# Two-block transformer, one core: the order of the first block's mixers, its output gates and its merge

## The chip, the cores and the metric

The kernel runs on one core of a Trainium2 chip, as one launch. The metric is the device time in microseconds (us) from the first to the last instruction, with what lies around it, of one execution; before the change the median of three runs is 3106.4 us. Five engines work side by side, each through its own instruction list, strictly in the order in which the program wrote it: TensorE (PE; its weight loads are shown apart as PEld), VectorE (DVE), ScalarE (ACT), GpSimd (POOL) and SyncE (SP, which issues the transfers).

## The reference, cut to what matters

The program computes two blocks of two layers each on 256 latent tokens of width 1024; the first block carries 256 context tokens as well. The change touches the token mixers of the first block alone:

```python
def token_mixers(hx, hc, ...):
    cu, mqkv, mo, mg, aq, ak, av, bg = split(h @ w_in)       # for latent and context tokens
    conv  = conformer_conv(cu, ...)      # a * sigmoid(g), 31 taps along the tokens, layernorm over 512 channels, silu, @ w_o
    mlstm = mlstm_readout(mlstm_bidirectional(...), mo, ...) # 4 heads of 256; rmsnorm per head, * sigmoid(mo), @ w_o
    attn  = attend(q, [k_c, k_x], [v_c, v_x]) @ w_attn_out   # 8 heads, 2 key heads
    g_conv, g_mlstm, g_attn = split(sigmoid(bg))
    return (g_conv * conv + g_mlstm * mlstm + g_attn * attn) @ w_out
```

Layer 0 needs latent and context outputs (512 columns), layer 1 only the latent ones (256). All arithmetic is float32.

## The kernel before

**Products.** Every float32 operand of a product is split into a high and a low half (fp32r), and each product is three matmuls: high by high, low by high, high by low. `lin` (L409 to L420) does this for one output tile of 128 features: it takes the next 128x128 weight pair from a stream and issues the three matmuls L417, L418 and L419 for each of kt tiles of the inner dimension (eight for the width of 1024). Activations lie feature by feature: 128 features in the partitions, the tokens (512 or 256) in the columns. Weights come as 512 KB transfers (`raw`), ACT makes the high half (`wh`, L326) and DVE the low half (`wl`, L310), 128x1024 at a time. A stream's order in memory is the order in which `lin` takes it, so the host packs it by `ORDER`.

**One layer of mixers.** After the normalisation come the gate logits, attention's keys, values and queries; then the loop over `ORDER`, which alternates m and c: for m, one mLSTM head (`mlstm`), for c, one quarter of the convolution's 512 channels (`glu_conv`). Behind them come eight more `lin` calls for the output gates (`mlstm_gate`), and then the merges: for each branch, 16 `lin` calls in layer 0 (eight for the branch's output product, eight for its merge gate).

- *An mLSTM head.* Q and k by `lin`, the score products L458 to L460 (`aux<-mq,mk` and the like), v by `lin`; then the head's 512 or 256 columns go through two segments of 256 (one in layer 1). A segment takes its forward and backward direction through two value blocks (`pv<-mv,mEh`, L1379 to L1381: 21 or 30 matmuls each), which need the decayed scores: PE (row maxima, `aux<-msr,selr`, L1337), ACT (an exponential), DVE (`mE<-...` and the low half `mEl`). DVE or ACT then brings the block out of PSUM as `mh` with a reciprocal; ACT squares `mh`, POOL takes the power of the mean and scales `mh` (L1321), PE transposes it (`aux<-cst,mh`, L1327) and it is stored in `hs`. There is one PSUM buffer for `pv` and one of each of the score operands.
- *A convolution quarter.* Two `lin` calls, ACT's tanh, DVE's product `glu<-glu,mm`, and then 31 taps on DVE: one multiplication (L319) and 30 multiply-adds (`cv<-glu,p,cv`, L307), each on the sum that the one before left. `conv_norm` takes the mean and the variance over the four quarters: POOL sums, PE multiplies by a constant (`aux<-ss,cst`, L1184), DVE subtracts (`cv<-aux,cv`).
- *Attention.* Scores, a softmax (DVE maxima, ACT exponentials, POOL scaling) and the value products L1138 (`aux<-pT,va`), in `ao`.

**What sets the order.** The program is written out by Python generators. `self.queue(name, interval, depth, generator)` puts side work into a named queue; `tick(us)`, which `lin` calls with its own nominal time, gives every queue that credit, and each time it reaches the interval one step of the queue's generator is written. So the interval says how far apart the steps stand in the engines' lists. `flush(name)` writes what is left at once. `soon()` marks work that is to be written early. Before the change attention's queue has an interval of 15.9 in layer 0, the convolution's 6.4, and a queue `ogate` multiplies `hs` by the output gates. The merges come in the order attention, convolution (flushed first), mLSTM.

The lines of the profile that matter here: L417 to L419 `lin`; L307 multiply-adds on DVE; L310 two-tensor operations on DVE; L326 high halves and L304 other passes on ACT; L313 and L321 on POOL.

Of the kernel before, what the change touches and what calls it, by code (L numbers as in the profile page):

```python
# [24 lines left out]
AF = mybir.ActivationFunctionType  # L25
OP = mybir.AluOpType
# [5 lines left out]
KD = D // P  # L32
# [4 lines left out]
MH = 4  # L37
# [24 lines left out]
ORDER = [(kind, h) for h in range(MH) for kind in "mc"]  # L62
# [111 lines left out]
def _layout(inp):  # L174
# [12 lines left out]
    for l in range(DEPTH):  # L187
        w = a["w_in"][l]
# [7 lines left out]
        for kind, h in ORDER:  # L196
            if kind == "m":
                c = slice(h * 256, (h + 1) * 256)
                parts += [qkv[:, :1024][:, c], qkv[:, 1024:2048][:, c]]
            else:  # L200
                parts += [cu[:, h * P:(h + 1) * P], cu[:, 512 + h * P:512 + (h + 1) * P]]
        parts.append(mo)
# [15 lines left out]
        g = a["mlstm_gate_b"][l]  # L218
# [73 lines left out]
class _K:  # L292
# [561 lines left out]
    def mixers(self, l, st, xs, segs, nq, first):  # L854
# [5 lines left out]
        with ExitStack() as es:  # L860
# [4 lines left out]
            with tc.tile_pool(name=f"head{l}", bufs=1) as hp:  # L865
# [19 lines left out]
                for j in range(4):  # L885
                    for seg in segs:
                        self.queue("attn", (15.9 if l == 0 else 15) * slow, 2 if l == 0 else 1, self.attention(j, seg, seg * len(segs) // 2, kT, va, hp, ao))
                for kind, h in ORDER:
                    if kind == "m":
                        self.mlstm(l, h, st, xs, xq, segs, nq, rows, hp, hs)  # L890
                    else:
                        self.queue("conv", (6.4 if l == 0 else 8.7) * slow, 1,
                                   self.glu_conv(l, h, st, xq, segs, nq, mp, cv), early=False)
                self.queue("conv", (6.4 if l == 0 else 8.7) * slow, 1, self.conv_norm(l, nq, cv))
                for n in range(0, KD, G):
                    self.mlstm_gate(l, n, st, xq, nq, hs)
                for name in ("mlstm", "ogate", "attn"):
                    self.flush(name)
                if l == 0:
                    self.load_x()  # L900
            with tc.tile_pool(name=f"merge{l}", bufs=1) as gp:
                merged = gp.tile([P, KD, nq], F32, name="merged")
                for name, src, kt, b, first in (("wba", ao, 4, 2, True), ("wbc", cv, 4, 0, False),
                                                ("wbm", hs, 8, 1, False)):
# [301 lines left out]
    def mlstm(self, l, h, st, xs, xq, segs, nq, rows, hp, hs):  # L1206
# [26 lines left out]
        with self.soon():  # L1233
            S = [self.mlstm_scores(seg, i * 256, qT, kT, hp) for i, seg in enumerate(segs)]
        nc.gpsimd.tensor_copy(v[0][:, :, 256:258], self.onec[:, None, :].to_broadcast([P, 4, 2]))
# [13 lines left out]
        for i, seg in enumerate(segs):  # L1249
            self.queue("mlstm", (6.8 if l == 0 else 5.8), 2, self.mlstm_seg(h, seg, i * 256, nq, S[i], v, rows, hp, hs))  # L1250

# [13 lines left out]
    def mlstm_gate(self, l, n, st, xq, nq, hs):  # L1265

        G = 512 // nq
        bank = self.mmt()
        for i in range(G):
            self.lin(bank[:, i * nq:(i + 1) * nq], st["wi"], xq, KD)  # L1270
        t = self.tmp()
        with self.soon():
            self.act(t, bank, AF.Tanh, scale=0.5)
            for i in range(G):
                w = self.mnwh[l][:, n + i:n + i + 1]
                self.act(t[:, i * nq:(i + 1) * nq], t[:, i * nq:(i + 1) * nq], AF.Identity, scale=w, bias=w)

        def finish():
            if n // 2 == 3:
                self.flush("mlstm")  # L1280
            m = hs[:, n:n + G, :].rearrange("p g n -> p (g n)")
            self.tt(m, m, t, OP.mult)
            yield

        self.queue("ogate", (5.2 if l == 0 else 6.9), 1, finish())
# [15 lines left out]
    def mlstm_seg(self, h, seg, c0, nq, S, v, rows, hp, hs):  # L1301
# [27 lines left out]
        nc.scalar.copy(hs[:, 2 * h:2 * h + 2, c0:c0 + 256], pt.rearrange("p (e q) -> p e q", e=2))  # L1329
# [458 lines left out]
```

## Time and profile before

| | |
|---|---|
| median of 3 runs (lowest to highest) | 3106.4 us (3102.4 to 3106.88) |
| the profiled execution: time, span | 3104.9 us, 3103.1 us |
| PE busy | 3044.2 us, 98% of the span |
| DVE, ACT, POOL busy | 60%, 47%, 12% |
| PE's mean granted clock | 0.995 of full speed |
| layer 0's mixers, first block | about 110 to 467 us |
| layer 1's mixers, first block | about 1190 to 1460 us |

A row of a timeline gives the start, the duration, the engine, the line and the operation as out<-in; in brackets stand the engine's idle time before it and what released it. A row of the groups by line gives the count, the busy time, the mean duration of one, and the idle time before. PE's records are pipelined: one matmul starts before the record of the last has ended, so a pace is read from starts. Records of consecutive DVE instructions overlap a little as well. [...]

### The profile page before, as it was taken

How to read it: one execution, taken by the hardware profiler on the slowest of the kernel's cores; microseconds unless marked ns; L12 is line 12 of the kernel's file. 1: busy time of each engine (PE TensorE's matmuls, PEld its weight loads, DVE VectorE, ACT ScalarE, POOL GpSimd, SP SyncE). 2: the span in 40 equal slices, each digit the busy share in tenths (PEclk: the TensorE clock that was granted, in tenths of full speed). 3: DMA queues.
4: the chain of work that ended last, by engine and by line, in shares of the span. 5: the costliest groups of instructions: out<-in, count | busy, mean ns of one | idle time of the engine just before them, and what ended most of it. 6: DMA issues, size and time to landing. Idle time of an engine off the chain costs nothing.

```text
span 3103.1 us, 52975 instructions
## 1 busy us (share of the span) xinstructions
PE 3044.2 (98%) x21432; PEld 2747.8 (89%) x21432; DVE 1872.4 (60%) x3093; ACT 1465.0 (47%) x2409; POOL 385.3 (12%) x397
## 2 busy tenths in 40 slices
PE   7999999999999999999999999999999999999999
PEld 5777778887777778899999999999999999999999
DVE  5477754335535546777587565576665665676664
ACT  4344454334323335556465544655544544654543
POOL 0211230113000032211110100122000000121000
PEclk9999989999999999999999999999999999999999
DMA  5433212324444433225555555444455555444553
GB/s 225 138 109 130 93 56 90 114 89 149 150 144 144 149 100 104 75 85 170 182 191 177 190 184 185 149 142 157 157 191 184 170 184 163 152 154 157 171 184 116
DMA packets 156134, 453.98 MB, mean 146 GB/s; under 512 B 14705, under 2 KB 57969, under 8 KB 154353
## 3 DMA queue, kind: packets, MB, share of 16 engines
q1 hardware_dynamic: 155168, 449.11, 44.4%
q8 instruction: 168, 2.75, 0.4%
q10 hardware_dynamic: 720, 1.49, 0.1%
q14 instruction: 78, 0.63, 0.1%
HBM read 447.13 MB, written 1.05 MB: 144 GB/s over the span
## 4 chain that ended last, share of the span: by engine, by line
PE 60%; POOL 0%; DMA 0%; DVE 0%; ACT 0%; issue 0%; SPq 0%; DVEq 0%; POOLq 0%
PE mm L417 16%; PE mm L419 16%; PE mm L418 16%; PE mm L452 1%; PE mm L453 1%; PE mm L451 1%; PE aux L372 1%; PE aux L1639 1%; PE mm L430 1%; PE mm L429 1%; PE mm L431 1%; PE aux L1619 1%; PE aux L506 0%; POOL ss L313 0%; PE aux L1138 0%; PE aux L1712 0%
## 5 line engine op out<-in xcount | busy, mean ns | idle before, releaser
L310 DVE TENSOR_TENSOR wl<-raw,wh 128x1024 fp32r<-128x1024 f32 x746 | 921.9, 1238 | 782.5 <-ACT wh L326 764.9
L326 ACT CAST wh<-raw 128x1024 fp32r<-128x1024 f32 x746 | 780.3, 1049 | 1095.8 <-PE mm L418 730.2
L417 PE MATMUL mm<-xh,wh 128*128 128x256 f32 (+1 forms) x3632 | 1126.5, 310 | 2.3 <-DVE xx L307 1.1
L419 PE MATMUL mm<-xh,wl 128*128 128x256 f32 (+1 forms) x3632 | 1126.5, 310 | 0.6 <-DVE gsm L975 0.6
L418 PE MATMUL mm<-xl,wh 128*128 128x256 f32 (+1 forms) x3632 | 1125.6, 310 | 0.0
L417 PEld LDWEIGHTS mm<-xh,wh 128*128 128x128 f32 x3632 | 689.5, 190 | 44.8 <-issue 8.7
L419 PEld LDWEIGHTS mm<-xh,wl 128*128 128x128 f32 x3632 | 689.6, 190 | 44.0 <-issue 9.3
L418 PEld LDWEIGHTS mm<-xl,wh 128*128 128x128 f32 x3632 | 689.8, 190 | 39.9 <-issue 6.8
L419 PE MATMUL mm<-ah,wl 128*128 128x256 f32 (+1 forms) x1056 | 317.5, 301 | 0.2 <-DVE wl L310 0.2
L418 PE MATMUL mm<-al,wh 128*128 128x256 f32 (+1 forms) x1056 | 317.6, 301 | 0.0
L417 PE MATMUL mm<-ah,wh 128*128 128x256 f32 (+1 forms) x1056 | 316.9, 301 | 0.0
L419 PEld LDWEIGHTS mm<-ah,wl 128*128 128x128 f32 x1056 | 200.9, 190 | 9.1 <-issue 2.1
L418 PEld LDWEIGHTS mm<-al,wh 128*128 128x128 f32 x1056 | 200.8, 190 | 9.1 <-issue 2.5
L417 PEld LDWEIGHTS mm<-ah,wh 128*128 128x128 f32 x1056 | 200.6, 190 | 8.7 <-issue 2.1
L313 POOL TENSOR_TENSOR small<-small,mhalf 128x2 f32<-128x2 f32 (+2 forms) x48 | 48.3, 1007 | 1075.4 <-DVE small L307 713.2
L307 DVE SCALAR_TENSOR_TENSOR cv<-glu,p,cv 128x512 f32<-128x512 f32 (+1 forms) x240 | 151.8, 633 | 3.4
L313 POOL TENSOR_TENSOR ss<-ss,t 128x256 f32<-128x256 f32 (+1 forms) x62 | 64.9, 1047 | 613.9 <-ACT t L304 593.3
L417 PE MATMUL mm<-bh,wh 128*128 128x512 f32 (+1 forms) x384 | 129.1, 337 | 2.5 <-ACT bh L326 1.5
L419 PE MATMUL mm<-bh,wl 128*128 128x512 f32 (+1 forms) x384 | 129.1, 337 | 0.3 <-DVE wl L310 0.3
L418 PE MATMUL mm<-bl,wh 128*128 128x512 f32 (+1 forms) x384 | 129.2, 337 | 0.0
L452 PE MATMUL mm<-wh,xl 128*128 128x256 f32 x448 | 127.8, 287 | 0.0
L453 PE MATMUL mm<-wl,xh 128*128 128x256 f32 x448 | 127.3, 286 | 0.0
(353 smaller groups left out, 4350.1 us busy)
## 6 DMA issues: line engine op xcount, KB each, us to landing
raw<-in_a_wup_dram SPq DMA_DIRECT2D x88, 512.0 KB, 3.4
raw<-in_b_f1u_dram SPq DMA_DIRECT2D x88, 512.0 KB, 3.7
raw<-in_b_f2u_dram SPq DMA_DIRECT2D x88, 512.0 KB, 3.7
araw<-in_ada_dram SPq DMA_DIRECT2D x80, 512.0 KB, 3.9
raw<-in_a_wi_dram SPq DMA_DIRECT2D x78, 512.0 KB, 3.4
raw<-in_b_wb_dram SPq DMA_DIRECT2D x72, 512.0 KB, 3.3
raw<-in_b_wi_dram SPq DMA_DIRECT2D x48, 512.0 KB, 3.4
raw<-in_a_wdn_dram SPq DMA_DIRECT2D x44, 512.0 KB, 3.4
```

The costliest lines, as they stand in the source:

```text
L307: self.nc.vector.scalar_tensor_tensor(out, in0, s, in1, op0=op0, op1=op1)
L310: self.nc.vector.tensor_tensor(out, in0, in1, op=op)
L313: self.nc.gpsimd.tensor_tensor(out, in0, in1, op=op)
L326: self.nc.scalar.copy(h, src)
L372: self.last_mm = self.nc.tensor.matmul(ps[0:32], x, x[:, 0:1].to_broadcast([P, 256]), start=True, stop=True).ins
L417: mm(ps, h, xh[:, k, cols], start=k == 0, stop=False)
L418: mm(ps, h, xl[:, k, cols], start=False, stop=False)
L419: self.last_mm = mm(ps, l, xh[:, k, cols], start=False, stop=k == kt - 1).ins
L429: mm(ps, h, xh[:, k, cols], start=k == 0 and i == 0, stop=False)
L430: mm(ps, h, xl[:, k, cols], start=False, stop=False)
L452: mm(ps, xl, w[0], start=False, stop=False)
L453: mm(ps, xh, w[1], start=False, stop=stop)
```

## The change

Four things change in the first block's mixers, and nothing elsewhere. First, layer 0's order becomes m0 c0 m1 c1 m2 m3 c2 c3 (it was m c m c m c m c), layer 1 keeps it; and before the quarters c2 and c3 are written, the convolution's queue is emptied down to one entry. Second, the eight output-gate `lin` calls go into the heads, two to each: before the head's v in heads 0 to 2, behind its queued segments in head 3. ACT writes the gate straight into `hs`, and the segment's end multiplies `hs` by the transposed `mh` from PSUM on DVE; ACT's 12 copies into `hs` go, and the 12 multiplications stay as many. The queue `ogate` is gone. Third, the intervals: attention 15.9 to 11.4 (layer 1: 15 to 12.5), convolution 6.4 to 8.0 (layer 1: 8.7 to 8.0). Fourth, the merges run attention, mLSTM, convolution. PE's instruction count is the same (20600), DVE's 3095 and POOL's 402 too, and ACT has 2268 instead of 2280. In the changed file `lin`'s matmuls are L418 to L420, DVE's L308 and L311, the value blocks L1374 to L1376, the transposes L1321, the row maxima L1332 and `conv_norm`'s product L1186.

```diff
+ORDER = [[("m", 0), ("c", 0), ("m", 1), ("c", 1), ("m", 2), ("m", 3), ("c", 2), ("c", 3)],
+         [("m", 0), ("c", 0), ("m", 1), ("c", 1), ("m", 2), ("c", 2), ("m", 3), ("c", 3)]]
...
-                        self.queue("attn", (15.9 if l == 0 else 15) * slow, 2 if l == 0 else 1, self.attention(j, seg, seg * len(segs) // 2, kT, va, hp, ao))
-                for kind, h in ORDER:
+                        self.queue("attn", (11.4 if l == 0 else 12.5) * slow, 2 if l == 0 else 1, self.attention(j, seg, seg * len(segs) // 2, kT, va, hp, ao))
+                conv = (8.0 if l == 0 else 8.0) * slow
+                for kind, h in ORDER[l]:
...
-                        self.queue("conv", (6.4 if l == 0 else 8.7) * slow, 1,
-                                   self.glu_conv(l, h, st, xq, segs, nq, mp, cv), early=False)
-                self.queue("conv", (6.4 if l == 0 else 8.7) * slow, 1, self.conv_norm(l, nq, cv))
-                for n in range(0, KD, G):
-                    self.mlstm_gate(l, n, st, xq, nq, hs)
-                for name in ("mlstm", "ogate", "attn"):
+                        if h > 1:
+                            while len(self.queues["conv"]["wait"] + self.queues["conv"]["live"]) > 1:
+                                self.step(self.queues["conv"])
+                        self.queue("conv", conv, 1, self.glu_conv(l, h, st, xq, segs, nq, mp, cv), early=False)
+                self.queue("conv", conv, 1, self.conv_norm(l, nq, cv))
+                for name in ("attn", "mlstm"):
                     self.flush(name)
...
-                for name, src, kt, b, first in (("wba", ao, 4, 2, True), ("wbc", cv, 4, 0, False),
-                                                ("wbm", hs, 8, 1, False)):
+                for name, src, kt, b, first in (("wba", ao, 4, 2, True), ("wbm", hs, 8, 1, False),
+                                                ("wbc", cv, 4, 0, False)):
...
             S = [self.mlstm_scores(seg, i * 256, qT, kT, hp) for i, seg in enumerate(segs)]
+        if h < MH - 1:
+            self.mlstm_gate(l, h, st, xq, nq, hs)
...
             self.queue("mlstm", (6.8 if l == 0 else 5.8), 2, self.mlstm_seg(h, seg, i * 256, nq, S[i], v, rows, hp, hs))
+        if h == MH - 1:
+            self.mlstm_gate(l, h, st, xq, nq, hs)
...
-        nc.scalar.copy(hs[:, 2 * h:2 * h + 2, c0:c0 + 256], pt.rearrange("p (e q) -> p e q", e=2))
+        m = hs[:, 2 * h:2 * h + 2, c0:c0 + 256]
+        self.tt(m, m, pt.rearrange("p (e q) -> p e q", e=2), OP.mult)
```

Three places show what moves. In the engines' lists `xN` is a run of equal instructions, and `aux`, `pv` and `mm` are PSUM tiles. The first is PE at the end of layer 0's mixers, up to the first matmul of the merges (`mm<-bh,wh`); before the change:

```order
L1123 MATMUL aux<-cst_69,t_4183 128x128 x4
L1123 MATMUL aux<-cst_69,t_4196 128x128 x4
L419 MATMUL mm<-xh,wl 128x512
...
L418 MATMUL mm<-xl,wh 128x512
L419 MATMUL mm<-xh,wl 128x512
L1138 MATMUL aux<-pT_3976,va 64x256
L1184 MATMUL aux<-ss,cst_69 128x512
L1138 MATMUL aux<-pT_3976,va 64x256 x7
L417 MATMUL mm<-bh,wh 128x512
L417 MATMUL mm<-xh,wh 128x512
```

After the change, from the last matmul of the last convolution quarter (the first row) on:

```order
L420 MATMUL mm<-xh,wl 128x512
L1374 MATMUL pv<-mv,mEh 128x258
...
L1376 MATMUL pv<-mv,mEl 128x258
L1321 MATMUL aux<-cst_69,mh 128x128
L1332 MATMUL aux<-msr,selr 128x256
...
L1321 MATMUL aux<-cst_69,mh 128x128 x4
...
L1321 MATMUL aux<-cst_69,mh 128x128 x2
L1186 MATMUL aux<-ss,cst_69 128x512
L1321 MATMUL aux<-cst_69,mh 128x128 x2
L418 MATMUL mm<-bh,wh 128x512
```

Before, `lin` matmuls (the output gates) stand between the pieces of attention right up to `conv_norm`'s product `aux<-ss,cst`. After, the last convolution quarter is the last `lin` of the mixers, and behind it PE has 102 value matmuls (blocks of 21, 30, 30 and 21), 16 transposes, 4 products for row maxima and `conv_norm`'s product, and then the merges.

The second is DVE in the same stretch, from the last quarter's `glu` to attention's low half `bl<-ao`, which the merges use first. Before:

```order
L307 SCALAR_TENSOR_TENSOR glu<-glu,mm 128x2x256
L307 SCALAR_TENSOR_TENSOR mE<-aux,gcols,cst_69 128x128 x2
...
L307 SCALAR_TENSOR_TENSOR cv<-glu,p_70,cv 128x512 x5
L310 TENSOR_TENSOR mod_82<-aux,p_70 128x8 x4
L307 SCALAR_TENSOR_TENSOR cv<-glu,p_70,cv 128x512
L307 SCALAR_TENSOR_TENSOR sc_0_6116<-mod_82,p_70 128x16
L307 SCALAR_TENSOR_TENSOR cv<-glu,p_70,cv 128x512
...
L307 SCALAR_TENSOR_TENSOR cv<-aux,cv 128x512 x4
L310 TENSOR_TENSOR hs<-hs,t_4305 128x512
L310 TENSOR_TENSOR bl<-ao,bh 128x512 x4
```

And after:

```order
L311 TENSOR_TENSOR wl<-raw,wh 128x1024
L308 SCALAR_TENSOR_TENSOR glu<-glu,mm 128x2x256
L308 SCALAR_TENSOR_TENSOR cv<-glu,p_70,cv 128x512
...
L308 SCALAR_TENSOR_TENSOR cv<-glu,p_70,cv 128x512 x2
L308 SCALAR_TENSOR_TENSOR mE<-aux,gcols,cst_69 128x128 x2
L308 SCALAR_TENSOR_TENSOR cv<-glu,p_70,cv 128x512 x2
...
L308 SCALAR_TENSOR_TENSOR cv<-glu,p_70,cv 128x512 x5
L311 TENSOR_TENSOR small<-small,gem 128x2
L1381 RECIPROCAL small<-small 128x2
L308 SCALAR_TENSOR_TENSOR mh<-pv,small,mh 128x256 x2
```

Before, some 70 rows of other work stand between the last tap and `cv<-aux`. After, 48 taps (17 of them of the quarter before) and 46 other instructions stand from `glu` to the last tap, and the last `mh`, which PE's last transposes need, comes behind the last tap; `cv<-aux` and `bl` follow it.

The third is PE in layer 1, around the transposes of the last head. Before:

```order
L418 MATMUL mm<-xl,wh 128x256
L1327 MATMUL aux<-cst_69,mh 128x128 x2
L419 MATMUL mm<-xh,wl 128x256
...
L417 MATMUL mm<-xh,wh 128x256
L1327 MATMUL aux<-cst_69,mh 128x128 x2
L418 MATMUL mm<-xl,wh 128x256
...
L419 MATMUL mm<-xh,wl 128x256
L417 MATMUL mm<-bh,wh 128x256
```

After, from the last matmul of the last value block (the first row) on:

```order
L1376 MATMUL pv<-mv,mEl 128x258
L419 MATMUL mm<-xl,wh 128x256
L420 MATMUL mm<-xh,wl 128x256
...
L419 MATMUL mm<-xl,wh 128x256
L420 MATMUL mm<-xh,wl 128x256
L1321 MATMUL aux<-cst_69,mh 128x128 x4
L418 MATMUL mm<-bh,wh 128x256
L418 MATMUL mm<-xh,wh 128x256
```

The transposes stood 77 `lin` matmuls behind the last value block; now eight stand between, and the merges begin right behind them.

In layer 0 the change also brings value blocks closer together: some 450 rows ahead of the place shown first, behind one value block of head 2, stand 4 small `araw` products, 4 of attention's value products and 4 transposes before the next value block, and behind that one 4 transposes, 4 attention scores and 4 `araw` products before the one after; no `lin` matmul stands in either gap.

## Rows read from the trace of the kernel before

**Rows 1.** The head of the page: span, and busy time of every engine.
```profile
span 3103.1 us, 52975 instructions
## 1 busy us (share of the span) xinstructions
PE 3044.2 (98%) x21432; PEld 2747.8 (89%) x21432; DVE 1872.4 (60%) x3093; ACT 1465.0 (47%) x2409; POOL 385.3 (12%) x397
```

**Rows 2.** Windows of layer 0's mixers, and one of layer 1: the columns stand first.
```profile
core 0: us, PE busy (x) PEld busy (x) DVE busy (x) ACT busy (x) POOL busy (x), PEclk, DMA share, GB/s
110.00:467.00 357.00, 342.11 (x2024) 269.89 (x2023) 238.58 (x479) 164.00 (x370) 79.97 (x69) 0.98 0.32 102
467.00:700.00 233.00, 232.03 (x1027) 191.31 (x1027) 86.93 (x103) 80.43 (x106) 26.13 (x21) 1.00 0.29 95
363.28:402.94 39.66, 34.85 (x199) 29.61 (x197) 38.82 (x82) 21.17 (x53) 12.58 (x9) 0.91 0.23 78
388.14:393.54 5.40, 5.40 (x25) 5.40 (x26) 4.86 (x11) 1.73 (x5) 2.67 (x2) 0.50 0.00 0
407.30:410.70 3.40, 3.40 (x10) 2.62 (x9) 2.28 (x7) 1.37 (x3) 0.30 (x1) 0.50 0.00 0
423.92:427.80 3.88, 3.88 (x18) 3.88 (x19) 2.55 (x6) 2.68 (x8) 2.45 (x3) 0.50 0.00 0
1190.31:1195.70 5.39, 5.39 (x16) 4.52 (x17) 2.89 (x7) 3.10 (x6) 2.77 (x4) 0.50 0.40 137
```

**Rows 3.** DVE's groups by line from 60 to 467 us.
```profile
L307 DVE SCALAR_TENSOR_TENSOR cv<-glu,p,cv 128x512 f32<-128x512 f32 x120 | 92.8, 774 | 1.3
L310 DVE TENSOR_TENSOR wl<-raw,wh 128x1024 fp32r<-128x1024 f32 x44 | 54.2, 1231 | 48.2 <-ACT wh L326 47.5 <-PE pv L1381 0.6
...
L310 DVE TENSOR_TENSOR mE<-mS,mE 128x768 f32<-128x768 f32 x4 | 3.8, 948 | 0.0
```

**Rows 4.** PE's groups by line in the same window.
```profile
L621 PE MATMUL aux<-araw,cpad 128*32 128x256 f32 x256 | 24.1, 391 | 2.8 <-DMA araw<-in_ada_dram 2.7
...
L1123 PE MATMUL aux<-cst,t 128*128 128x128 f32 x96 | 16.1, 281 | 0.7 <-ACT hs L1329 0.6
...
L1337 PE MATMUL aux<-msr,selr 100*128 100x256 f32 x16 | 5.1, 319 | 1.4 <-ACT t L304 0.9 <-DVE small L317 0.5
L1327 PE MATMUL aux<-cst,mh 128*128 128x128 f32 x32 | 5.0, 276 | 0.0
```

**Rows 5.** PE's timeline around the two longest waits of layer 0.
```profile
381.67 0.28 PE L1380 MATMUL pv<-xc,mEh 128*128 128x256 f32 x1
381.79 0.29 PE L1381 MATMUL pv<-mv,mEl 128*128 128x258 f32 x1
...
388.14 0.58 PE L1379 MATMUL pv<-mv,mEh 128*128 128x258 f32 x1 [4.57 <-ACT mh L304]
388.52 0.41 PE L1380 MATMUL pv<-xc,mEh 128*128 128x256 f32 x1
388.74 0.42 PE L1381 MATMUL pv<-mv,mEl 128*128 128x258 f32 x1
...
418.17 0.28 PE L1381 MATMUL pv<-mv,mEl 128*128 128x258 f32 x1
...
423.92 0.55 PE L1379 MATMUL pv<-mv,mEh 128*128 128x258 f32 x1 [4.41 <-DVE mh L307]
```

**Rows 6.** An mh of DVE in layer 0, and the transposes behind it.
```profile
395.50 0.87 DVE L307 SCALAR_TENSOR_TENSOR mh<-pv,small,mh 128x256 f32<-128x256 f32 x2
...
398.97 0.95 PE L1327 MATMUL aux<-cst,mh 128*128 128x128 f32 x6
```

**Rows 7.** Layer 1: last value matmul, DVE's mh and the first transposes.
```profile
1396.36 0.28 PE L1381 MATMUL pv<-mv,mEl 128*128 128x258 f32 x1
...
1397.93 0.87 DVE L307 SCALAR_TENSOR_TENSOR mh<-pv,small,mh 128x256 f32<-128x256 f32 x2
...
1405.71 0.38 PE L1327 MATMUL aux<-cst,mh 128*128 128x128 f32 x2
```

More of the change, by code (lines that the diff above doesn't have):

```diff
@@ L58, in _chunks @@
     return [min(size, n - i) for i in range(0, n, size)]
-ORDER = [(kind, h) for h in range(MH) for kind in "mc"]
+ORDER = [[("m", 0), ("c", 0), ("m", 1), ("c", 1), ("m", 2), ("m", 3), ("c", 2), ("c", 3)],
+         [("m", 0), ("c", 0), ("m", 1), ("c", 1), ("m", 2), ("c", 2), ("m", 3), ("c", 3)]]
 STREAMS1 = {
@@ L195, in _layout @@
         parts = [gates, ak[:, rows[:P]], av, aq[:, rows][:, head]]
-        for kind, h in ORDER:
+        for kind, h in ORDER[l]:
             if kind == "m":
                 c = slice(h * 256, (h + 1) * 256)
-                parts += [qkv[:, :1024][:, c], qkv[:, 1024:2048][:, c]]
+                parts += [qkv[:, :1024][:, c], qkv[:, 1024:2048][:, c], mo[:, c]]
             else:
                 parts += [cu[:, h * P:(h + 1) * P], cu[:, 512 + h * P:512 + (h + 1) * P]]
-        parts.append(mo)
         s1["wi"].append(_pack(_fan(_blocks(np.concatenate(parts, axis=1)), NFIRST), STREAMS1["wi"]))
@@ L886, in mixers @@
                     for seg in segs:
-                        self.queue("attn", (15.9 if l == 0 else 15) * slow, 2 if l == 0 else 1, self.attention(j, seg, seg * len(segs) // 2, kT, va, hp, ao))
-                for kind, h in ORDER:
+                        self.queue("attn", (11.4 if l == 0 else 12.5) * slow, 2 if l == 0 else 1, self.attention(j, seg, seg * len(segs) // 2, kT, va, hp, ao))
+                conv = (8.0 if l == 0 else 8.0) * slow
+                for kind, h in ORDER[l]:
                     if kind == "m":
@@ L1263, in pair, with mlstm_gate @@
             yield slice(i, i + 1), q[:, None, :]
[L1265 to L1285, printed above, removed]
+    def mlstm_gate(self, l, h, st, xq, nq, hs):
+        for sl, ps in self.pair(st, xq, nq):
+            with self.soon():
+                t = hs[:, 2 * h:2 * h + 2, :][:, sl, :]
+                self.act(t, ps, AF.Tanh, scale=0.5)
+                for i in range(2)[sl]:
+                    w = self.mnwh[l][:, 2 * h + i:2 * h + i + 1]
+                    self.act(hs[:, 2 * h + i, :], hs[:, 2 * h + i, :], AF.Identity, scale=w, bias=w)
     def mlstm_scores(self, seg, c0, qT, kT, hp):
```

## The prediction

> **What bounds the kernel now.** I read the head of the page first: PE is busy for 98% of the span and DVE for 60% [rows 1], so time is won only where PE stands still or runs at half its clock, and lost where the change makes it do so. The windows come next, since an average over 3103 us says little of a change that touches two stretches. Layer 0's mixers are the place: from 110 to 467 us PE is busy 342.1 of 357.0 us, so it stands still for 14.9 us, while over the merges that follow (467 to 700 us) it stands still for 1.0 us [rows 2]. PE's timeline names the two long waits, 4.57 us and 4.41 us, both of a value block for `mh` of the block before it [rows 5]. [...] All that any reordering of layer 0's mixers can win is therefore 14.9 + 6.3 = 21.2 us. The last thing to see is DVE from 363.28 us, the last quarter's `glu`, to 402.94 us, its last tap: 38.82 of 39.66 us busy with 82 instructions [rows 2]. There DVE is the slow engine; PE does not stop only because other matmuls are in its list.
>
> **The end of layer 0's mixers.** PE executes the same number of matmuls, so the sum is one of idle time and clock. Let T0 be the end of the last quarter's `lin` matmuls, the first row of the changed list. Behind T0 PE has 102 value matmuls at 0.12 us from start to start, 12.2 us [rows 5], 16 transposes at 5.0/32 = 0.16 us and 4 row maxima at 5.1/16 = 0.32 us [rows 4], and one product for `conv_norm` that I take as two of these: 16.5 us together. Then the merges' first matmul stands behind the last transposes, and these behind the last `mh`.
>
> On DVE, `glu` to the last tap is 48 taps and 46 others, one behind the other. The stretch from 363.28 to 402.94 us had 31 taps and 51 others. With 0.774 us for a tap [rows 3] its others took (39.66 - 24.0)/51 = 0.307 us each, and the new stretch takes 37.2 + 46 x 0.307 = 51.3 us. Four of those others were weight splits of 1.23 us [rows 3], of which the new stretch has none; without them an other takes 0.229 us and the sum is 47.7 us. The new one has more long pieces of the value blocks' scores (948 ns for 768 columns [rows 3]), so I take the middle, 49.5 us, with 47.7 and 51.3 as ends. Before `glu` DVE may still have the two taps and one split that stand right ahead of it, nothing to 2.8 us; I take 1.4. Behind the last tap come two small instructions (0.3 us) and `mh`, and from the start of `mh` to the transposes it took 3.5 us in layer 0 [rows 6] and 7.8 us in layer 1 [rows 7]; I take layer 0's. From T0 to PE's restart: 1.4 + 49.5 + 0.3 + 3.5 = 54.7 us, of which PE fills 16.5. **Idle: 38.2 us** (35.0 to 45.4). In the kernel before the same taps lay beside eight `lin` calls of the output gates and attention; the change moves both ahead of T0, and that cover is what is gone. Putting the convolution last in the merges does not bring it back: in DVE's list all taps stand ahead of `bl<-ao`, and in PE's the convolution's first product stands ahead of the merges, whichever branch they begin with.
>
> The trace has a row for the tap, 774 ns for 512 columns [rows 3]. [...]
>
> **The place where PE starts again.** After an idle stretch PE's granted clock is 0.50 for 5.40 and 3.88 us in layer 0 and for 5.39 us in layer 1 [rows 2]; the merges then begin at that rate and lose half of 5.4, **2.7 us** (nothing to 2.7).
>
> **Ahead of T0.** Value blocks share one PSUM buffer, and from the last matmul of one to the first of the next it took 388.14 - 381.91 = 6.2 and 423.92 - 418.29 = 5.6 us [rows 5]. In the changed list two such turnarounds of head 2 have only small products between them: 4 `araw` at 24.1/256 = 0.09, 4 value products at 0.12 and 4 transposes at 16.1/96 = 0.17, together 1.5 us; and 4 transposes, 4 scores (a guess of 0.25 each, twice a value matmul) and 4 `araw`, 2.1 us [rows 4, 5]. With 5.9 us for a turnaround the waits are 4.4 and 3.8 us: **8.2 us** (nothing, if a split or a tap less stands before `mh`, to 12). The clock after them I take as after the two long waits before, half of 5.40 and 3.88: **4.6 us** [rows 2].
>
> **What goes.** All waits and half-rate stretches before, 21.2 us, are taken as gone, since the value blocks and row maxima that wait there lie elsewhere now. That is the most that can go. The 12 copies on ACT that go, and attention's shorter interval, I price at nothing: PE's `lin` work covers them ahead of T0, and ACT is busy 164 of 357 us [rows 2]; were the copies on the path, 12 of them at DVE's 0.774 us for that width [rows 3] would be worth 9 us, which lies within the range.
>
> **Layer 1.** From the last value matmul to the first transposes it took 1405.71 - 1396.36 = 9.35 us [rows 7]. 77 `lin` matmuls lay there; eight are left, at 0.12 us, and the merges are behind the transposes: 9.35 - 0.12 - 1.0 = **8.2 us** idle and another **2.7 us** of half rate, 10.9 us (nothing, if the transposes find `mh` ready, to 12). In layer 1 the taps do lie beside the merges, since `conv_norm` is written into them.
>
> **The sum.** 38.2 + 2.7 + 8.2 + 4.6 - 21.2 = 32.5 us in layer 0, and 10.9 in layer 1: 43.4 us on the profiled execution's 3104.9 us, 3148.3 us. The median of the runs shown is 1.5 us above that execution, so 3150 us in their measure.
>
> **The rivals.**
> - *Only the tail.* The stalls ahead of T0 and in layer 1 don't come, because ACT and DVE are ahead of PE there, and only the tail is paid: 38.2 + 2.7 - 21.2 = 19.7 us, 3126 us. For it: the same chain in layer 1 was covered entirely before. Against: in the list of after, only eight matmuls cover it. 0.17.
> - *A slower tail.* [...] 0.10.
> - *Nothing to measure.* PE's work is unchanged, and idle time only moves from the two waits to the end. The new idle time would have to be 21 us in both layers together, so DVE would have to be through its stretch in about 30 us. [...] 39.66 us for 31 taps speaks against it [rows 2]. 3106 us, 0.05.
> - *Faster.* One mechanism: the taps of the last two quarters run beside the merges, where DVE is busy only 86.9 of 233 us [rows 2], and PE goes from the last `lin` straight into attention's merge. Then there is no tail, and the 21.2 us go: 3085 us. It decides if DVE reaches `bl<-ao` within about 37 us of T0 (16.5 + 21.2). Against: DVE's list has all the taps ahead of it. 0.06.
>
> **How the numbers follow.** The forecast has a chance of 0.62, 3150 us; its own range is 3135 to 3165, from the ends of the tail (-3 and +7), of the waits ahead of T0 (-8 and +4) and of layer 1 (-11 and +1), not all at once. The range of 3120 to 3170 takes in the first two rivals and leaves out the other two and a part of the outer ones. What a measurement here can tell from no change is 0.2%, 6.2 us. Faster has 0.06, no change 0.04 (the third rival without its outer part), slower 0.90.
>
> **What the new profile would show.** If the steps are right: a PE gap or a row of gaps of 35 to 45 us in total just before the merges of layer 0, with DVE over 95% busy there and the row before the first merge matmul waiting for `mh` or the transposes; PE's clock at 0.50 in it; a gap of about 8 us before the merges of layer 1; and the long waits at 388 and 424 us replaced by two near each other, earlier than T0. The forecast is wrong if DVE has idle time over 10% in that tail, if PE's merges begin while taps still run in layer 0, or if the span less PE's busy time, 58.9 us before [rows 1], is under 80 us after.

## The result, and the profile after

The changed kernel takes 3140.2 us in the median of 4 runs (3138.1 to 3144.1), against 3105.7 us of the kernel before beside it: 34.4 us more, a ratio of 1.0114 (95% interval 1.0097 to 1.0132). The forecast was 3150 us. The profiled execution has a span of 3142.4 us, 39.3 us above the one before. The head of its page, which answers to [rows 1]:

```profile
span 3142.4 us, 52980 instructions
## 1 busy us (share of the span) xinstructions
PE 3061.2 (97%) x21432; PEld 2758.1 (88%) x21432; DVE 1876.5 (60%) x3093; ACT 1460.8 (46%) x2397; POOL 379.6 (12%) x397
```

PE has as many instructions as before and 17.0 us more busy time; the other 22.3 us of the 39.3 are idle time. One mark of PE's timeline tells the layers apart. The wait that opens layer 1's mixers stood at 1190.31 us [rows 2]; it now stands here:

```profile
1222.85 0.47 PE L1025 MATMUL aux<-cst,t 128*128 128x128 f32 x1 [6.72 <-POOL t L1021]
```

So layer 0 gives 1222.85 - 1190.31 = 32.5 us, and what comes behind the other 6.8 us. Not all of the 32.5 us are the change's. PE's list is the same in both kernels up to one matmul near 120 us, which comes first from the trace before and then from the changed kernel's:

```profile
117.57 0.39 PE L419 MATMUL mm<-xh,wl 128*128 128x512 f32 x1
```
```profile
120.37 0.39 PE L420 MATMUL mm<-xh,wl 128*128 128x512 f32 x1
```

2.8 us were lost before the two lists differ at all, by a difference between two executions of the same work; from there on layer 0 is 29.7 us longer. The windows of the changed kernel, in order: up to the last quarter; from the last `lin` matmul (T0) to the merges' first matmul; the dense part of that tail; and PE's start in the merges. They answer to [rows 2]; PEclk is the granted clock as a share of full speed.

```profile
core 0: us, PE busy (x) PEld busy (x) DVE busy (x) ACT busy (x) POOL busy (x), PEclk, DMA share, GB/s
110.00:440.00 330.00, 328.01 (x1936) 254.28 (x1934) 187.85 (x377) 146.26 (x315) 61.74 (x58) 1.00 0.33 107
436.20:496.60 60.40, 29.16 (x126) 24.04 (x125) 53.19 (x104) 18.00 (x52) 17.44 (x14) 0.62 0.12 44
443.80:481.30 37.50, 18.09 (x71) 15.46 (x71) 37.43 (x74) 11.75 (x36) 8.49 (x7) 0.50 0.00 1
491.60:501.80 10.20, 8.00 (x18) 5.39 (x19) 5.48 (x9) 2.18 (x4) 2.17 (x3) 0.50 0.12 51
```

Up to 440 us PE hardly stands still (330.0 - 328.0 = 2.0 us) at full clock: the two waits of [rows 5] are gone. What PE loses in layer 0 from 110 us on to waits and half rate lies in the tail of 60.4 us and the restart behind it. In the tail PE is busy for 29.2 us, 18.1 us of them in the dense part at a granted clock of 0.50, while DVE is busy for 53.2 us (88%), and for 37.4 of 37.5 us in the dense part. The restart at 496.60 us still runs at 0.50 until 501.8 us. What PE waited for in the tail (total, times, longest):

```profile
PE pv L1374 <- ACT mEh L327: 8.3, 2, 6.3
PE aux L1321 <- POOL mh L1315: 7.9, 4, 4.2
PE pv L1374 <- ACT mh L305: 6.6, 2, 3.7
PE pv L1374 <- DVE mh L308: 4.9, 1, 4.9
PE pv L1376 <- DVE mEl L311: 1.6, 2, 0.9
```

No wait names the convolution: PE waits for the operands of the value blocks, for `mh` and for POOL's scaling of it. DVE's timeline gives the stretch forecast: the last quarter's `glu`, the last five taps, and what follows.

```profile
438.68 0.68 DVE L308 SCALAR_TENSOR_TENSOR glu<-glu,mm 128x512 f32<-128x512 f32 x1
...
483.42 3.88 DVE L308 SCALAR_TENSOR_TENSOR cv<-glu,p,cv 128x512 f32<-128x512 f32 x5
489.01 0.16 DVE L311 TENSOR_TENSOR small<-small,gem 128x2 f32<-128x2 f32 x1 [1.71 <-ACT small L305]
...
495.45 2.48 DVE L308 SCALAR_TENSOR_TENSOR cv<-aux,cv 128x512 f32<-128x512 f32 x4 [4.32 <-PE aux L1186]
```

From 438.68 to 487.30 us it is 48.6 us.

### The profile page after: what moved, and what is told of

It is laid out like the page before. It is cut to its first block, busy times and chain, and to the rows that moved or that the text cites. A ratio compares the mean times of both kernels' runs of the same rounds, so it can differ in the third digit from the quotient of the medians.

```text
span 3142.4 us, 52980 instructions
## 1 busy us (share of the span) xinstructions
PE 3061.2 (97%) x21432; PEld 2758.1 (88%) x21432; DVE 1876.5 (60%) x3093; ACT 1460.8 (46%) x2397; POOL 379.6 (12%) x397
## 4 chain that ended last, share of the span: by engine, by line
PE 59%; issue 1%; DVE 0%; DMA 0%; ACT 0%; POOL 0%; SPq 0%; DVEq 0%; POOLq 0%; ACTq 0%
PE mm L418 16%; PE mm L420 16%; PE mm L419 16%; PE mm L453 1%; PE mm L452 1%; PE mm L454 1%; PE mm L431 1%; PE mm L432 1%; PE aux L373 1%; PE mm L430 1%; PE aux L1634 1%; PE aux L1614 1%; PE aux L507 0%; PE aux L1140 0%; PE aux L1707 0%
## 5 line engine op out<-in xcount | busy, mean ns | idle before, releaser
L311 DVE TENSOR_TENSOR wl<-raw,wh 128x1024 fp32r<-128x1024 f32 x746 | 921.5, 1238 | 793.9 <-ACT wh L327 775.5
L418 PE MATMUL mm<-xh,wh 128*128 128x256 f32 (+1 forms) x3632 | 1128.4, 311 | 1.5 <-DVE xx L308 1.1
L420 PE MATMUL mm<-xh,wl 128*128 128x256 f32 (+1 forms) x3632 | 1127.9, 311 | 0.6 <-DVE gsm L977 0.6
L418 PEld LDWEIGHTS mm<-xh,wh 128*128 128x128 f32 x3632 | 690.7, 190 | 44.2 <-issue 9.2
L420 PEld LDWEIGHTS mm<-xh,wl 128*128 128x128 f32 x3632 | 690.8, 190 | 43.9 <-issue 8.6
L420 PE MATMUL mm<-ah,wl 128*128 128x256 f32 (+1 forms) x1056 | 317.5, 301 | 0.2 <-DVE wl L311 0.2
L418 PE MATMUL mm<-ah,wh 128*128 128x256 f32 (+1 forms) x1056 | 317.0, 301 | 0.0
L420 PEld LDWEIGHTS mm<-ah,wl 128*128 128x128 f32 x1056 | 200.9, 190 | 9.1 <-issue 2.1
L418 PEld LDWEIGHTS mm<-ah,wh 128*128 128x128 f32 x1056 | 200.6, 190 | 8.7 <-issue 2.1
L308 DVE SCALAR_TENSOR_TENSOR cv<-glu,p,cv 128x512 f32<-128x512 f32 (+1 forms) x240 | 149.8, 630 | 3.6
L418 PE MATMUL mm<-bh,wh 128*128 128x512 f32 (+1 forms) x384 | 129.7, 339 | 2.3 <-ACT bh L327 1.4
L420 PE MATMUL mm<-bh,wl 128*128 128x512 f32 (+1 forms) x384 | 129.0, 337 | 0.3 <-DVE wl L311 0.3
L452 PE MATMUL mm<-wh,xh 128*128 128x256 f32 x448 | 125.8, 287 | 0.0
```

Source lines behind the costliest of these rows:

```text
L308: self.nc.vector.scalar_tensor_tensor(out, in0, s, in1, op0=op0, op1=op1)
L311: self.nc.vector.tensor_tensor(out, in0, in1, op=op)
L418: mm(ps, h, xh[:, k, cols], start=k == 0, stop=False)
L420: self.last_mm = mm(ps, l, xh[:, k, cols], start=False, stop=k == kt - 1).ins
L452: mm(ps, xh, w[0], start=start, stop=False)
```

## The experiments

Each is compared with the kernel before on the same chip; the medians of that kernel beside them lie between 3103.7 and 3107.1 us, and each ratio is against its own. Theory A of the expectations is the prediction's, in two halves: DVE's taps bind the tail (E1), and what binds it does so because the `lin` calls of the gates no longer cover it (E2, E3, E5, E7). Theory C, from E8 on, is that attention's pieces were the cover. "L0" is the shift of layer 1's opening wait against 1190.31 us, "rest" what is left of the difference in span; both are of one profiled execution, which can stand some us off the median. At the matmul near 120 us up to which PE's lists agree, the shift is already +2.8 us in the changed kernel and in E11, +2.6 in E3, +2.4 in E10, -2.2 in E2 and -2.7 in E7, and at most 0.4 in the others; "from the common point" below means L0 less this. The tail is the time from the last `lin` matmul of layer 0's mixers to the merges' first matmul, and "values" the value matmuls in it.

| kernel | median us | ratio (95% interval) | L0 | rest | tail us | values |
|---|---|---|---|---|---|---|
| before | 3105.9 | 1 | 0 | 0 | 5 | 0 |
| changed | 3140.2 | 1.0114 (1.0097 to 1.0132) | +32.5 | +6.8 | 60.4 | 102 |
| E1 few taps | 3124.2 | 1.0061 (1.0046 to 1.0076) | +16.5 | +5.5 | 42.9 | 81 |
| E2 gates behind | 3137.3 | 1.0104 (1.0089 to 1.0119) | +29.6 | +1.5 | 0.2 | 0 |
| E3 order back | 3140.9 | 1.0108 (1.0090 to 1.0126) | +28.8 | +7.1 | 68.8 | 120 |
| E4 merge order back | 3168.9 | 1.0208 (1.0190 to 1.0225) | +46.5 | +17.2 | as changed | as changed |
| E5 before, new intervals and merge order | 3124.7 | 1.0065 (1.0053 to 1.0077) | +17.5 | +2.4 | 0.2 | 0 |
| E6 before, attention's interval alone | 3123.5 | 1.0067 (1.0055 to 1.0080) | +17.6 | +2.3 | 0.2 | 0 |
| E7 late gates | 3132.1 | 1.0090 (1.0075 to 1.0104) | +20.9 | +0.8 | 49.2 | 81 |
| E8 attention's interval undone | 3110.9 | 1.0017 (1.0008 to 1.0026) | +4.0 | +4.8 | 37.8 | 42 |
| E9 E8 and late gates in layer 1 | 3110.5 | 1.0013 (1.0004 to 1.0022) | +4.7 | +1.1 | 36.4 | 42 |
| E10 E9 and head 3's late gate in layer 0 | 3111.5 | 1.0018 (1.0009 to 1.0027) | +9.8 | -1.0 | 41.6 | 51 |
| E11 E9 with interval 18 | 3097.7 | 0.9976 (0.9967 to 0.9985) | -1.1 | -2.0 | 19.2 | 0 |

**E1, few taps.** What it leaves out stands in the expectation.

```diff
-        for k in range(31):
+        for k in range(1 if l == 0 and j > 1 else 31):
```

> The changed kernel, but the last two convolution quarters of layer 0 take only their first tap of 31: 60 of layer 0's 120 multiply-adds are left out, so the output is another. Theory A, DVE's taps set the tail: from the last lin matmul to the merges' first matmul it took 59.7 us with DVE 99% busy; without the taps what is left is the value blocks' own chain, four blocks and three turnarounds of 3.4 us (as ahead of the last quarters) and 5 us at the end, about 35 us, so the kernel takes about 25 us less: 3115 us (3108 to 3122). Theory B, the value blocks' chain sets the tail and the taps only fill its waits: the turnarounds stay near 6 to 7 us, the tail stays over 50 us, and the kernel takes 3130 to 3140 us.

Measured: 3124.2 us, between the two, so neither theory holds whole. (The 99% of the expectation is right for the dense part alone; over the whole tail of the changed kernel DVE is busy for 88%.) The first row is the tail, the second its value matmuls alone:

```profile
437.90:480.80 42.90, 24.16 (x102) 19.84 (x100) 21.45 (x55) 15.98 (x49) 9.82 (x10) 0.66 0.11 40
```
```profile
437.90:480.80 42.90, 17.75 (x81) 16.18 (x81) 2.63 (x6) 3.50 (x12) 0.66 0.11 40
```

DVE's load is half the time now (21.5 of 42.9 us), and the tail still takes 42.9 us with 81 value matmuls. Leaving the taps out shortened the tail by 17.5 us and the kernel by 16.0 us, but the written order moved with them, and 21 value matmuls fewer stand in the tail; what the taps alone are worth is not separated. E7 has 81 value matmuls as well, with 24 taps in its tail, and takes 49.2 us; its gates lie elsewhere too, so the 6 us between them is no measure of the taps either. What is shown is that most of the tail stays without them: theory A is wrong as the whole cause.

**E2, gates behind.** All gates behind the last quarter, with `mlstm_gate` (here `late_gate`), ACT's copies, the queue `ogate` and the order of flushes of the kernel before.

```diff
+LATE = [(0, 1, 2, 3), (0, 1, 2, 3)]
...
-                parts += [qkv[:, :1024][:, c], qkv[:, 1024:2048][:, c], mo[:, c]]
+                parts += [qkv[:, :1024][:, c], qkv[:, 1024:2048][:, c]] + ([] if h in LATE[l] else [mo[:, c]])
...
+        parts += [mo[:, h * 256:(h + 1) * 256] for h in LATE[l]]
...
+                for h in LATE[l]:
+                    for n in range(2 * h, 2 * h + 2, G):
+                        self.late_gate(l, n, st, xq, nq, hs)
```

> The changed kernel with one part undone: all output gates behind the last quarter again, in both layers (with the copies on ACT), order, intervals and merge order as changed. Theory A, the tail is long because no lin stands behind the last quarter: eight lin calls of 5.46 us are 43.7 us of cover for a tail of 59.7 us with 16.5 us of PE's own work, so the tail's loss goes almost wholly, layer 1's 6 us too, and the time comes to 3098 to 3112 us. Rival, the order m2 m3 c2 c3 itself makes the loss (two quarters' taps on DVE at the end): the loss only moves behind the gates and the time stays above 3120 us.

Measured: 3137.3 us. The rest falls to +1.5 us, as expected of layer 1, but layer 0 hardly. There is no tail: the loss sits ahead of the gates' last `lin` calls, which the written order put behind the last head's value blocks, and in waits for the transfers (`araw`) of layer 0's own modulation weights, whose products are written in between:

```profile
PE aux L625 <- DMA araw<-in_ada_dram: 8.0, 6, 3.7
PE pv L1405 <- ACT t L308: 4.4, 1, 4.4
PE aux L1349 <- POOL mh L1343: 4.3, 3, 3.0
```

So as a test of cover it did not put the cover where the waits are, and the rival's number came out without its mechanism being shown. E7 tests cover better.

**E3, order back.**

```diff
-ORDER = [[("m", 0), ("c", 0), ("m", 1), ("c", 1), ("m", 2), ("m", 3), ("c", 2), ("c", 3)], ...
+ORDER = [[(kind, h) for h in range(MH) for kind in "mc"]] * 2
```

> The changed kernel with one part undone: layer 0 in the order m c m c m c m c again; gates stay inside the heads, merges and intervals as changed. Theory A (cover behind the last head is missing; DVE's taps lengthen the tail): only one quarter, 10.9 us of lin, stands behind the last head instead of two, but 17 taps fewer are left for the tail; the tail stays at 40 to 60 us with 14 to 20 us of PE work, and the time is 3120 to 3145 us. Rival, the order alone is at fault: the time falls to 3112 us or less.

Measured: 3140.9 us, as theory A had it: the order m2 m3 c2 c3 alone is not the cause. The tail is longer, with more value matmuls in it:

```profile
424.30:493.10 68.80, 40.37 (x199) 33.32 (x197) 50.13 (x112) 26.59 (x79) 12.90 (x13) 0.72 0.11 39
```
```profile
424.30:493.10 68.80, 26.22 (x120) 23.27 (x120) 3.49 (x8) 4.73 (x16) 0.72 0.11 39
```

**E4, merge order back.**

```diff
-for name, ... in (("wba", ...), ("wbm", ...), ("wbc", ...)):
+for name, ... in (("wba", ...), ("wbc", ...), ("wbm", ...)):
```

> The changed kernel with one part undone: merges in the order attention, convolution, mLSTM again. All theories of the tail: the first merge waits for the transposes of the last head in either order, so layer 0 stays within 5 us, 3136 to 3146 us. Rival (the merge order matters, since the convolution merged second would have to wait for its norm): 3146 us or more.

Measured: 3168.9 us, 29 us above the changed kernel; by the profiled executions 14 us of it lie in layer 0 (16 from the common point) and 10 behind it. All theories of the tail missed it; the rival named it. The first two rows are of layer 0's merges, the third of layer 1's:

```profile
568.88 1.87 PE L507 MATMUL aux<-cst,ss 128*128 128x1 f32 x8 [6.56 <-POOL ss L314]
...
577.02 0.79 PE L418 MATMUL mm<-bh,wh 128*128 128x512 f32 x1 [3.79 <-ACT bh L327]
...
1509.63 1.01 PE L507 MATMUL aux<-cst,ss 128*128 128x1 f32 x4 [4.77 <-POOL ss L314]
```

PE stops in both layers for the sums of `conv_norm`'s variance, which cannot begin before the taps and the mean are done. With taps this late, the convolution merged last is worth 29 us; in the kernel before, it and the convolution's interval together change nothing (E5 against E6).

**E5, the kernel before with the new intervals and merge order.**

```diff
-self.queue("attn", (15.9 if l == 0 else 15) * slow, ...
+self.queue("attn", (11.4 if l == 0 else 12.5) * slow, ...
...
-self.queue("conv", (6.4 if l == 0 else 8.7) * slow, ...
+self.queue("conv", 8.0 * slow, ...
...
-for name, ... in (("wba", ...), ("wbc", ...), ("wbm", ...)):
+for name, ... in (("wba", ...), ("wbm", ...), ("wbc", ...)):
```

> The kernel before with two parts of the change alone: its intervals (attention 11.4 and 12.5, convolution 8.0) and its merge order (attention, mLSTM, convolution); the order m c m c m c m c and the output gates behind the last quarter stay as before. Theory A (the loss comes from taking the lin calls of the gates from behind the last head): in PE's list every value block of the last head now stands between lin matmuls and attention has ended by then, so the two waits of 4.57 and 4.41 us and most of the 21.2 us of layer 0 go and nothing is lost: 3086 to 3100 us. Rival (the new intervals or the merge order cost time by themselves): 3106 us or more.

Measured: 3124.7 us, against 3103.7 us beside it. The theory fell: parts that I had priced at nothing cost 20 us where neither gates nor order are moved.

**E6, the kernel before with attention's interval alone.**

```diff
-self.queue("attn", (15.9 if l == 0 else 15) * slow, ...
+self.queue("attn", (11.4 if l == 0 else 12.5) * slow, ...
```

> The kernel before with one part of the change alone: attention's interval (11.4 in layer 0, 12.5 in layer 1). Theory: this interval alone moves attention ahead, and the gates' lin calls come free for the value blocks; the taps end before the merges here, so that the merge order and the convolution's interval do not matter: within 4 us of the kernel with all three, 3086 to 3102 us. Rival (the merge order is what helps): 3104 us or more, as before.

Measured: 3123.5 us, the same as E5: the whole cost is this interval's, the rival named the wrong part. PE's two longest sums of waits there, and three windows, up to the merges and two at half rate:

```profile
PE aux L621 <- DMA araw<-in_ada_dram: 8.4, 4, 3.7
PE pv L1379 <- ACT mh L304: 5.4, 2, 3.2
```
```profile
110.00:484.50 374.50, 352.94 (x2025) 276.46 (x2024) 241.27 (x480) 164.00 (x369) 76.38 (x69) 0.94 0.28 94
318.70:335.80 17.10, 13.90 (x53) 7.17 (x54) 14.10 (x30) 5.86 (x19) 7.21 (x5) 0.50 0.46 154
445.00:458.70 13.70, 8.90 (x37) 7.94 (x36) 8.95 (x25) 10.19 (x28) 2.56 (x3) 0.50 0.00 1
```

PE stands still for 21.6 us instead of 14.9, and in the last two windows alone 22.8 us of its work run at a granted clock of 0.50, which loses 11.4 us by the clock where the kernel before lost 6.3 in all. More waits between value blocks and for transfers, and the half rate around them, are this loss.

**E7, late gates.** Gates of heads 2 and 3 behind the last quarter in both layers; the segments' ends wait in the writing.

```diff
+LATE = [(2, 3), (2, 3)]        # heads whose gates are written behind the last quarter
...
+        while h not in self.gated:
+            yield
```

> The changed kernel, but the output gates of heads 2 and 3 are written behind the last quarter, in both layers, and their segments' ends wait for them; all else as changed. Theory A (missing cover): four lin calls more stand behind the quarters, 21.8 us in layer 0, the blocks without lin between them fall from 102 matmuls in four to 60 in two, and layer 1 has 57 lin matmuls behind the last block instead of eight: the time falls by 15 to 33 us, to 3107 to 3125 us. Rival (the chain of the last two heads is set by its own buffers, whatever stands between): 3128 us or more, with layer 1's 6 us gone at the most.

Measured: 3132.1 us, with 3124.8 us of span in the profiled execution, the fastest of its runs. The tail, its value matmuls, and layer 1's transposes and first merge matmul:

```profile
436.00:485.20 49.20, 23.57 (x101) 19.14 (x99) 34.22 (x73) 15.79 (x46) 11.04 (x11) 0.64 0.09 32
```
```profile
436.00:485.20 49.20, 17.09 (x81) 15.43 (x81) 2.62 (x6) 2.50 (x9) 0.64 0.09 32
```
```profile
1435.90 0.44 PE L1330 MATMUL aux<-cst,mh 128*128 128x128 f32 x2 [0.61 <-POOL mh L1322]
...
1438.01 0.39 PE L421 MATMUL mm<-bh,wh 128*128 128x256 f32 x1 [1.67 <-ACT bh L330]
```

The time is the rival's (3128 us or more), not theory A's. 81 value matmuls are left, not 60. L0 falls by 11.6 us, but by only 6.2 us from the common point, and the medians differ by 8.0 us in both layers together: as cover for layer 0's tail, two heads' gates are worth some us and not the loss. In layer 1 the wait of 4.52 us is 0.61 us and the rest falls from +6.8 to +0.8 us: there the missing `lin` matmuls are the cause.

**E8, attention's interval undone.**

```diff
-self.queue("attn", (11.4 if l == 0 else 12.5) * slow, ...
+self.queue("attn", (15.9 if l == 0 else 15) * slow, ...
```

> The changed kernel with one part undone: attention's interval 15.9 in layer 0 and 15 in layer 1 again; order, gates inside the heads, convolution's interval and merge order as changed. Theory C (attention's shorter interval takes attention's pieces away from beside the last heads' value blocks; this alone cost the kernel before 20 us): in PE's list attention's last products and transposes now stand between the last two value blocks, two blocks of 21 are left without lin instead of four with 102, and 16 taps come behind the merges' first split, so layer 0 loses no more than before (within -8 and +6 us of it) and layer 1 keeps its 6 us: 3102 to 3116 us. Theory A alone (the missing lin calls are the cause, attention is too small to matter): 3128 us or more.

Measured: 3110.9 us, as theory C had it. This interval gives back 29 of the 34 us, with gates, order and merges as changed. In the profiled executions layer 0 gives 28.5 us of it (32.5 - 4.0; 26.2 from the common point). The tail and its value matmuls:

```profile
430.20:468.00 37.80, 18.12 (x91) 11.42 (x89) 33.37 (x63) 10.86 (x32) 10.83 (x8) 0.78 0.12 42
```
```profile
430.20:468.00 37.80, 6.80 (x42) 6.41 (x42) 1.74 (x4) 1.37 (x5) 0.78 0.12 42
```

The last `lin` matmul comes 6 us earlier, since more of attention is left for later, and behind it stand 42 value matmuls instead of 102; attention's pieces fill PE instead, from 444.6 to 453.0 us without a wait.

**E9, E8 with late gates in layer 1.**

```diff
+LATE = [(), (2, 3)]
```

> As the kernel with attention's interval undone, and in layer 1 alone the output gates of heads 2 and 3 behind the last quarter, so that 50 lin matmuls instead of eight stand behind the last value block. If layer 1's cost is the uncovered chain of the last head, this is 6 us faster than that kernel (4 to 8): 3096 to 3110 us. Rival (layer 1's cost comes from the intervals): the same within 2 us.

Measured: 3110.5 us. In the profiled executions the rest falls from +4.8 to +1.1 us, nearly as expected; the medians differ by 0.4 us, inside their spread of several us, which is what the rival had. The runs alone don't show it.

**E10, E9 with head 3's gate in layer 0 late.**

```diff
+LATE = [(3,), (2, 3)]
```

> As the last one, and head 3's output gate in layer 0 behind the last quarter too, so that two lin calls, 10.9 us, lie beside the value blocks instead of ahead of them. If lin cover still limits, 3 to 8 us faster than the last one; if the chain of value blocks limits whatever stands between, the same within 3 us.

Measured: 3111.5 us, the same: the two `lin` calls moved did not come to lie between the last value blocks (51 are left in the tail, not fewer).

**E11, E9 with attention's interval 18.**

```diff
-self.queue("attn", (15.9 if l == 0 else 15) * slow, ...
+self.queue("attn", (18 if l == 0 else 15) * slow, ...
```

> As the kernel with attention's interval undone and layer 1's late gates, but attention's interval in layer 0 is 18 instead of 15.9. Theory C (what stands behind the last lin matmuls decides: value blocks wait for each other, attention's pieces do not): in PE's list all value blocks of the last two heads now stand between lin matmuls and only attention's last products, transposes and one head's transposes are left behind, while 29 taps lie beside the merges; layer 0 then loses 3 to 10 us instead of the 21.2 us of the kernel before, and the time falls below it: 3086 to 3100 us. Rival (DVE's taps, or the merges that start beside them, cost what the tail no longer does): 3104 us or more.

Measured: 3097.7 us, inside theory C's range, 0.24% under the kernel before and the fastest of all. From the common point layer 0 is 3.9 us shorter than before. No value matmul stands in the tail, and PE's waits from 110 to 470 us are few:

```profile
443.50:462.70 19.20, 9.99 (x46) 5.33 (x44) 17.66 (x29) 6.39 (x14) 4.98 (x4) 0.76 0.09 28
```
```profile
443.50:462.70 19.20, 0.00 (x0) 0.00 (x0) 0.00 (x0) 0.00 (x0) 0.76 0.09 28
```
```profile
PE aux L1131 <- POOL t L1123: 5.8, 2, 4.4
PE aux L1131 <- ACT t L308: 1.8, 1, 1.8
PE mm L421 <- ACT bh L330: 1.0, 1, 1.0
```

Over E3, the changed kernel, E7, E10, E8 and E11 the tail falls with the value matmuls left in it: 120, 102, 81, 51, 42, 0 give 68.8, 60.4, 49.2, 41.6, 37.8, 19.2 us. The taps in these tails, 30, 49, 24, 42, 36 and 21, show no such order. The tail's length is not the loss, since PE's own work in it differs: E3 has the longest tail, with 40.4 us of busy PE against 29.2 us in the changed kernel, and shifts layer 0 by 28.8 us against 32.5. The convolution's new interval was not undone in the changed kernel; without attention's new interval all other parts of the change cost 5 us together (E8).

## Why the prediction was right, and where it was not

**The tail of layer 0: size nearly right, cause half right.** Forecast 54.7 us from T0 to the merges, measured 60.4 us. The sum over DVE's list held (49.5 against 48.6 us). What follows the last tap was too small, 3.8 against 496.60 - 487.30 = 9.3 us: DVE waited 1.71 us for ACT, and the last transposes and `conv_norm`'s product stood behind `mh` at a granted clock of 0.50. Less PE's 16.5 us of work, 43.9 us are lost, where I had 38.2 (the upper end of that term, 45.4 us, adds up to 45.7). But that the taps bound it was too simple. DVE's list and the value blocks' chain run side by side; with the taps gone 42.9 us stayed (E1). A full DVE did not show that DVE decides.

**The signs named ahead.** By one of its own signs the forecast was wrong: DVE was to be idle for no more than 10% of the tail and was idle for 7.2 of 60.4 us, 12%. PE's gaps there were to be 35 to 45 us and are 31.2. Two long waits near each other were to come ahead of T0; they are 0.66 and 0.85 us. The half rate in the tail came as named, and the span less PE's busy time is 81.2 us, just above the 80 named.

**The step that failed: attention's interval, priced at nothing.** The prediction said that PE's `lin` work covers it. E8 shows that undoing it gives back 29 of the 34 us. At 11.4 attention is written out early, the value blocks of the last two heads are left for the end, and these wait for one another. The prediction saw that attention had been cover, but priced the cover by the gates' `lin` calls; putting those of two heads back behind the last quarter gives some 6 us of layer 0 (E7). The parts do not add: the interval costs 20 us in the kernel before (E6) and 29 us in the changed one, and the rest of the change 5 us at the old interval and 15 us at the new one (34.4 - 19.7). E6 shows that the interval costs 18 us in layer 0 without any tail, with 8.4 us of waits for transfers of layer 0's own modulation weights, more between value blocks, and PE's work at half rate around them; why these transfers come late there stays open.

**Ahead of T0: 12.8 us forecast, 2.0 us measured.** The turnaround of 5.9 us was read where DVE was full (7.88 of 8.00 us from 381 us on); from 345 to 356 us of the changed kernel it is busy for 7.69 of 11.00 us. There, at the two turnarounds of head 2:

```profile
345.48 0.28 PE L1376 MATMUL pv<-mv,mEl 128*128 128x258 f32 x1
...
349.17 0.39 PE L1374 MATMUL pv<-mv,mEh 128*128 128x258 f32 x1 [0.66 <-DVE mh L308]
...
351.64 0.28 PE L1376 MATMUL pv<-mv,mEl 128*128 128x258 f32 x1
...
355.02 0.39 PE L1374 MATMUL pv<-mv,mEh 128*128 128x258 f32 x1 [0.85 <-ACT mh L305]
```

From the start of a block's last matmul to the next block it is 3.7 and 3.4 us, and 2.9 and 2.4 us of small products fill it; the waits are 0.66 and 0.85 us, and the clock stays at 1.00.

**PE's restart: right.** 2.7 us forecast; 0.50 from 496.60 to 501.80 us loses 2.6 us.

**What goes: 21.2 us.** Of these, 14.9 us are PE's idle time from 110 to 467 us, and 6.3 us are half of the 12.7 us (5.40, 3.40 and 3.88) that it worked at a granted clock of 0.50 [rows 2]; there the value matmuls start some 0.22 us apart, against 0.12 at 1.00 [rows 5]. With the measured terms layer 0 is 43.9 + 2.0 + 2.6 - 21.2 = 27.3 us, and it shifted by 32.5 us. Of the 5.2 us between, 2.8 were lost ahead of the common point and are not the change's. The other 2.4 are not in any wait; I did not settle where they lie. So the 32.5 us forecast for layer 0 came out right by luck, by errors that cancel: the tail 5.7 too small, the part ahead of T0 10.8 too large, 5.2 not seen.

**Layer 1: 10.9 us forecast, 6.8 measured.** The mechanism is as forecast (E7, E9), but the chain is shorter than the 9.35 us read from [rows 7]:

```profile
1445.45 0.28 PE L1376 MATMUL pv<-mv,mEl 128*128 128x258 f32 x1
...
1451.21 0.69 PE L1321 MATMUL aux<-cst,mh 128*128 128x128 f32 x2 [4.52 <-POOL mh L1315]
...
1453.60 0.58 PE L418 MATMUL mm<-bh,wh 128*128 128x256 f32 x1 [0.57 <-ACT bh L327]
```

It took 5.76 us. The 9.35 us of the kernel before were not the chain's: PE was busy all that time with the `lin` matmuls that stand ahead of the transposes (77 at 0.12 us are 9.2 us), and the transposes then did not wait.

```profile
1396.36:1405.71 9.35, 9.35 (x81) 9.35 (x79) 8.50 (x18) 6.72 (x14) 4.07 (x3) 1.00 0.43 141
```

So [rows 7] gave an upper end and no length for the chain.

**The rivals.** A tail without the other stalls had its part in layer 0, where the stalls ahead of T0 did not come. A slower tail, with the value blocks at half their clock and DVE waiting for them, was right in its first half: PE's clock is 0.50 for the whole dense part, and the value matmuls start some 0.21 us apart there; its second half did not come, since DVE was busy for 37.4 of those 37.5 us. Nothing to measure and faster are refuted by 1.0097 as the lower end of the ratio. The share of the most occupied engine alone is no measure of the 34 us or of E11's gain: PE is busy for 98% of the span before and 97% after, and from 110 to 697 us for 97% before (572.1 of 587.0 us) and 98% in E11 (577.3).

## What to carry to other kernels

In a program with a fixed order per engine, ask of the last work before a barrier whether its pieces wait for one another: a serial chain belongs between the large matmuls and independent pieces belong at the end, not the other way round. A pacing constant that adds and removes no instruction can weigh more than the code that is moved with it; price it by what it leaves behind the last cover. That an engine is full beside a chain doesn't show that it is the bound: take its work away and see what stays. Before a shift between two traces is put down to a change, look at the last point at which their lists still agree.

## What was not expected of the hardware

With half of DVE's time free, PE's clock stayed low through the tail (0.66 in E1's 42.9 us, 0.62 in 60.4 us with the taps); PE stands still in both, for 18.7 and 31.2 us. The value matmuls of the dense part start some 0.21 us apart, the pace of [rows 5] at 0.50, instead of 0.12, so that the blocks themselves take longer beside the waits: the block of 21 that starts at 444.87 us takes 4.5 us from its first start to its last, the one at 436.49 us, at 1.00, 2.4 us. That the clock is low because PE stands still was not tested; the traces show the two side by side. In E4 the merges slowed alike: behind PE's wait for the variance's sums the `lin` matmuls of 512 columns start 0.43 us apart (577.61 to 579.74 us), ahead of it 0.23 us.
